# State-space stage: three sums per step made by DMAs that add to their destination

## The chip, the cores and the metric

The kernel runs on one core of a Trainium2 chip. It is one launch. The metric is the time of the launch in microseconds of the device, as the median of several runs. Five engines work side by side, each through its own queue of instructions in order: PE (TensorE, matrix products), DVE (VectorE), ACT (ScalarE), POOL (GpSimd) and SP (SyncE, which here only issues DMAs). 16 DMA engines move data between DRAM and the on-chip memory.

## The reference

Two layers over 1024 latent tokens and 256 context tokens of 1024 features, all float32. The first layer is a diagonal state-space mixer in both directions, the second an attention; each is followed by a SwiGLU block. The change lies in the mixer:

```python
def s5_direction(u, h0, ar, ai, bbr, bbi, C_re, C_im, reverse, want_y):
    ug = u.reshape(Bn, L, S5_G, S5_GC).swapaxes(0, 1)      # 64 groups of 16 features
    br = jnp.einsum('lbgc,gpc->lbgp', ug, bbr)             # 64 complex states a group
    bi = jnp.einsum('lbgc,gpc->lbgp', ug, bbi)
    ...                                                    # the state h0 of the context enters
    _, _, hr, hi = lax.associative_scan(s5_combine, (a_r, a_i, br, bi), reverse=reverse, axis=0)
    y = (jnp.einsum('lbgp,gcp->blgc', hr, C_re) - jnp.einsum('lbgp,gcp->blgc', hi, C_im))
```

## The kernel before

Features lie on the partitions, tokens along the free axis. Tokens are taken in blocks of eight: 160 blocks, J = 160, the first 32 of them context. Within a block the mixer is a matrix product; from block to block it is a scan of complex states. The complex scan is made a real one: the block inputs are turned back by the angle of their block (tables "tcs" and "tsn", cosine and sine), scanned with a real factor, and the states are turned forward again.

The loop of the stage has 32 steps (NS5) of two groups, both directions. A step n works at several depths at once:

- PE makes the block inputs of step n + 2 (`in_products`, tile psA, from the tokens "ug" and the input stack "bt").
- DVE runs the six scans of step n (`scans`: tile "zz" from "ww"), then turns the inputs of step n + 2 (`in_turn`: the products "pc" and "pq" of psA with the two tables), does one pass on the tables of step n + 3 (`ty`), turns the states of step n forward (`turn_back`: "qc", "qs") and makes the output stack "sc" of step n + AHEAD, AHEAD = 8 (`stack_out`: two products "sc", "su" and their difference).
- POOL adds pc and pq to "ww" (`in_sum`) and makes the input stack "sb" of step n + 4 (`stack_in`: two products "sb", "su" and their sum).
- ACT makes the tables (`tables_a`, `tables_c`: "ty", "tn", "tsn", "tcs"), and copies what PE wrote (`out_copy`: "gy"; `turned`: "bt").
- PE makes the outputs of step n - 1 (`out_products`, from qc, qs, sc, its swapped copy "cw", "ug" and "mt"), and transposes sb of step n + 3 (`turned`).
- SP loads and stores; every fourth step it loads the tokens ug of the next four steps (`load_u`), into one of two buffers.

The scan of the second direction needs the first column of ww behind the last one as well. Therefore ww has J + 1 columns, and ACT copies that pad column after POOL's sum:

```python
    def in_sum(pq):
        w = gt.tile([128, 4, J + 1], F32, name="ww", bufs=NW)
        add(w[:, :, :J], pq[0], pq[1], Q)
        copy(w[:, 1::2, J:J + 1], w[:, 1::2, 0:1])
```

From the first step on, the five queues keep the order in which the program is written (`pinned.update("VSQTD")`; V, S, Q, T, D are DVE, ACT, POOL, PE and SP). Before the loop a scheduler sets the order. All engine instructions are issued through one wrapper, so the profile shows the same line, L197, for all of them; they are told apart by the names of their tiles.

Of the kernel before, what the change touches and what calls it, by code (L numbers as in the profile page):

```python
"""Hybrid S5 / latent-attention trunk: two layers, one launch.

Everything is kept feature-major (features on partitions, tokens on the free
axis), so that no activation is ever transposed between products.  Tokens are
ordered (token-in-block t = 0..7, block j): 32 context blocks, then 128 latent
blocks, which gives the state-space mixer its blocks of eight tokens.

Float32 products with long moving operands are carried as three passes over
an exact two-part split of both operands (12 + 12 significant bits).
"""  # L10
# [46 lines left out]
# ---------------------------------------------------------------- host layout  # L57
def _units(w):
    """[K, N] -> [N/128][128 p][K/128 * 128]: one contiguous block per output tile."""
    k, n = w.shape  # L60
    return np.ascontiguousarray(
        w.reshape(k // 128, 128, n // 128, 128).transpose(2, 1, 0, 3)).reshape(n // 128, 128, k)
# [7 lines left out]
def _rope_rows():  # L70
    """cos and signed sin for the 32 rotary rows, for the latent tokens in kernel order."""
# [13 lines left out]
def _constants():  # L85
# [3 lines left out]
    steps = np.stack([j, np.where(j < JC, JC - 1 - j, J - 1 + JC - j)]).astype(np.float32)  # L89
    k["idx"] = np.broadcast_to(steps.reshape(1, 2 * J), (128, 2 * J))  # L90
# [91 lines left out]
# -------------------------------------------------------------------- device  # L182
def trunk(tc, I, out, dbg=None):
# [4 lines left out]
    class Engine:  # L188
        """an engine whose instructions keep the order of the program while pinned"""
# [31 lines left out]

    def split(h, l, x):
        """x -> (h, l): h = x rounded to 12 bits, l = the rest, both exact."""
        S.activation(h, x, AF.Copy)
        V.tensor_tensor(l, x, h.bitcast(F32), op=ALU.subtract)

    def split_in(h, l, e):
        """l holds the f32 values; split in place"""
        l32 = l.bitcast(F32)
        copy(h, l32)  # L230
        sub(l, l32, h.bitcast(F32), e)
# [43 lines left out]
    class Weights:  # L275
        """The weights of a sequence of products, loaded and split ahead of their use, in blocks
        of up to four tiles [128, 128].  A spec is ((one matrix [128, n * 128],), n), taken whole,
        or ((two of them), n), taken block by block in the order of `seven`."""
# [42 lines left out]
        def combined(self, s, j, w):  # L321
            """a11, a12, s2, a22, s3, s1, s4 with s1 = a21 + a22, s2 = s1 - a11, s3 = a11 - a21,
            s4 = a12 - s2"""
# [23 lines left out]
    def weights(specs):  # L347
        """a function that returns the weights in turn"""
        ws, ns = Weights([((ap,), n) for ap, n in specs]), iter(specs)
        return lambda: ws.whole(next(ns)[1])  # L350

    def mm3(outs, w, xs, nk, ks=None):
        """outs[n] += sum_k w[k]^T x[k][n], float32 in three passes; xs(k, n) -> (h, l)."""
# [7 lines left out]
    # ---------------------------------------------------------- constants  # L361
# [48 lines left out]
    def single(pst):  # L410
        """one bank after the other of the tiles of pst"""
        while True:
            t = pst()
            for n in range(t.shape[1]):
                yield t[:, n]

    # ------------------------------------------------------------- norms
# [3 lines left out]
    def rstd_of(acc, dim, ncol, nsub, pst, r=None):  # L421
        """1/sqrt(mean of squares + eps) per token on every partition; acc holds the squares,
        summed over feature tiles"""
# [15 lines left out]
    # a value that the next norm waits for  # L439
    behind_of = []  # L440

    def modnorm(p, xs, ncol, nsub, ranges, l, half, put, pst, nb=3, spare=None, order=range(8)):
        """in pieces: four for the squares, one for the mean, eight for the features;
        with eight spare tiles, in place and without memory of its own"""
# [30 lines left out]
    def put_seven(p, h, new, w):  # L475
        """of the tiles ft and ft + 4, halved along the tokens: b11, t1, b21, b22, t2, t3, -t4 with
        t1 = b12 - b11, t2 = b22 - t1, t3 = b22 - b12, t4 = t2 - b21"""
# [21 lines left out]
    # the products of `seven`: which of the combinations of put_seven takes part  # L499
# [27 lines left out]
    # ================================================ layer 0: S5 mixer  # L527
# [21 lines left out]
    def mod_first(st):  # L549
        """shift and scale of the first norm, on the tensor engine"""  # L550
# [26 lines left out]
    def discretise(st):  # L577
# [12 lines left out]
        def tanh_exp(o, x):  # L590
            """exp(x) = (1 + tanh(x/2)) / (1 - tanh(x/2))"""
# [62 lines left out]
        for o, x in zip(cpw, (pr, pi)):  # L654
            copy(by_d(o, 0), by_d(x, 0)[:, 1:9])
            V.tensor_copy(by_d(o, 1), by_d(x, 1)[:, 8:0:-1])
# [42 lines left out]
    def w_in_norm(p, xc):  # L699
        """normalised in place; in pieces"""  # L700
# [67 lines left out]
    idx = const("idx", 2 * J, sp)  # L768
# [16 lines left out]
    AHEAD = 8  # L785

    def stack(k, name, p_, x1, x2, op, e, p, nb):
        """for two groups, both directions: powers times coefficients"""
# [8 lines left out]
        u = ge.tile(sh, F32, name="su", tag="su" + name, bufs=1)  # L797
# [3 lines left out]
        e.tensor_tensor(a, a, u, op=op)  # L801
        return a.rearrange("p g t c -> p g (t c)")

    def stack_in(k):
        """with B-bar"""
        k0 = 4 * k
        sbs[k] = stack(k, "sb", bp, bb1[:, k0:k0 + 4], bb2[:, k0:k0 + 4], ALU.add, Q, ge, 2)

    def stack_out(k):
        """with C"""  # L810
        c = coef[k // 2][:, :, 4 * (k % 2):4 * (k % 2) + 4]
        scs[k] = stack(k, "sc", cpw, c[:, 0], c[:, 1], ALU.subtract, V, gp, 10), c[:, 0]

    def swap(k):
        """the latter with its halves swapped"""
# [6 lines left out]
    def turned(k):  # L822
        """the former, transposed; the lag kernels, by four groups"""
# [28 lines left out]
    def lag_out(q):  # L852
        """the products within a block"""
# [12 lines left out]
    def load_u(ft):  # L866
        ug = gp.tile([128, 8, J], F32, name="ug")
        dma(ug, ubd[ft].rearrange("t c g j -> (t c) g j"))
# [4 lines left out]
    NPC, NW, NGY = 2, 2, 2  # L873
    sh4 = [128, 4, J]

    def tables_a(n):
        """turns of two groups, both directions"""
        ty = wp.tile([128, 1024], F32, name="ty", tag="wr")[:, :4 * J].rearrange("p (a b) -> p a b", a=4)
        tn = wp.tile([128, 1024], F32, name="tn", tag="wb", bufs=6)[:, :4 * J].rearrange("p (a b) -> p a b", a=4)
        for i in range(4):  # L880
            S.activation(ty[:, i], idx[:, (i % 2) * J:(i % 2) * J + J], AF.Copy, scale=f8[:, 4 * n + i:4 * n + i + 1])
# [7 lines left out]
    def tables_c(n):  # L889
        """rotation tables"""  # L890
        ty, tn = tys.pop(n)
        tcs = gp.tile(sh4, F32, name="tcs", bufs=4)
        tsn = gp.tile(sh4, F32, name="tsn", bufs=4)
        trig(tcs, tsn, ty, tn, sg[:, 2:3])
        tab[n] = tcs, tsn

    def beside(m):
# [4 lines left out]
        if m == 4:  # L902
            for k in range(2):
                stack_in(k)
                stack_out(k)
                turned(k)
# [3 lines left out]
        if m == 6:  # L910
            for k in range(2, 4):
                stack_in(k)
                stack_out(k)
            turned(2)
# [8 lines left out]
        if m == 7:  # L923
            for k in range(4, AHEAD):
                stack_out(k)

# [4 lines left out]
    def in_products(n):  # L931
        """inputs of two groups (both directions) to the block states"""
        bt, ug = bts.pop(n), ugs[n // 4]
        va = []
        for sw in range(2):
            v = psA()
            for i in range(4):
                T.matmul(v[:, i // 2, (i % 2) * J:(i % 2) * J + J], bt[:, i, 64 * sw:64 * sw + 128],
                         ug[:, (2 * n + i // 2) % 8], start=True, stop=True)
# [3 lines left out]
    def in_turn(n, va):  # L943
        """rotated"""
        pq = []
        for v, t, nm in zip(va, tab[n], ("pc", "pq")):
            p_ = gt.tile(sh4, F32, name=nm, tag=nm, bufs=NPC)
            mul(p_.rearrange("p (g d) j -> p g (d j)", g=2), v[:, :, :2 * J],
                t.rearrange("p (g d) j -> p g (d j)", g=2))
            pq.append(p_)  # L950
        return pq

    def in_sum(pq):
        w = gt.tile([128, 4, J + 1], F32, name="ww", bufs=NW)
        add(w[:, :, :J], pq[0], pq[1], Q)
        copy(w[:, 1::2, J:J + 1], w[:, 1::2, 0:1])
# [5 lines left out]
    def scans(n, w, z):  # L962
        """over the blocks"""
# [5 lines left out]
        for i in (1, 3):  # L969
            scan(z[:, i, 0:JC - 1][:, ::-1], w[:, i, 1:JC][:, ::-1], i, 0.0)  # L970
        for i in (0, 2):
            scan(z[:, i, 1:J], w[:, i, 0:J - 1], i, 0.0)
        for i in (1, 3):
            scan(z[:, i, JC:J][:, ::-1], w[:, i, JC + 1:J + 1][:, ::-1], i, z[:, i, 0:1])

    def turn_back(n, z):
        qc = gt.tile(sh4, F32, name="qc", bufs=2)
        qs = gt.tile(sh4, F32, name="qs", bufs=2)
        mul(qc, z, tab[n][0])
        mul(qs, z, tab[n][1])  # L980
        return qc, qs

    def out_products(n, rot):
# [3 lines left out]
        for gi in range(2):  # L987
            o = py[:, gi * J:gi * J + J]
            T.matmul(o, mt[:, (2 * n + gi) % 4], ug[:, (2 * n + gi) % 8], start=True, stop=False)
# [18 lines left out]
    # steps of two groups; a step works on its scans, on the inputs two steps ahead, on the tables  # L1008
    # three steps ahead, on the stacks three and four steps ahead, and on the outputs one behind
    NS5 = 32  # L1010
    pend = {}
    for n in range(2):
        pend[n] = in_sum(in_turn(n, in_products(n)))
    rot = None
    pinned.update("VSQTD")
    for n in range(NS5 + 1):
# [16 lines left out]
        if n + 2 < NS5:  # L1033
            pq = in_turn(n + 2, va)
# [10 lines left out]
        if n + 4 < NS5:  # L1045
            stack_in(n + 4)
        if n + AHEAD < NS5:
# [3 lines left out]
        if n + 2 < NS5:  # L1051
            pend[n + 2] = in_sum(pq)
# [20 lines left out]
    def raw_y(ft):  # L1073
        """in the place of the residual stream"""
# [10 lines left out]
    # ==================================== layer 0: GLU, out projection  # L1085
# [7 lines left out]
    # the other modulation rows: on the vector engine, from rows of mod_w^T  # L1093
# [103 lines left out]
    # ============================================================== FFN  # L1197
# [681 lines left out]
```

## Time and profile before

| | before |
|---|---|
| runs | 3453.87, 3454.31, 3463.31 us |
| median | 3454.31 us |
| span of the profiled execution | 3461.5 us |
| PE busy | 3205.4 us (93%) |
| DVE busy | 2857.2 us (83%) |
| ACT busy | 1746.7 us (50%) |
| POOL busy | 1107.7 us (32%) |
| stage with the loop, 187 to 524 us | 337 us: DVE 331.1, PE 243.7, POOL 216.6, ACT 169.3 us busy |

The profile gives for the profiled execution its span, from the first to the last instruction, and no further time of its own. Shares over the whole span are shares over stages that differ: outside the loop PE is nearly always busy (2812.8 of the 2937 us behind it), inside it is not. So the stage is read by itself.

### The profile page before, as it was taken

The page shows a single profiled execution, that of the slowest core. Times are in us where ns is not written, and L with a number is a line of the kernel's source. Part 1 is how long each engine was busy: PE and PEld are TensorE (multiplying, and loading weights), DVE is VectorE, ACT ScalarE, POOL GpSimd, SP SyncE. Part 2 cuts the span into 40 slices and gives each one's busy share as a digit, 9 for nine tenths or more (in the row PEclk, how much of TensorE's full clock was granted, in tenths as well). Part 3 has the DMA queues.
Part 4 walks back from the last instruction along what each step waited for, and adds up shares of the span by engine and source line. Part 5 has one row for each costly group of instructions (what it writes and reads, how often), then busy time and mean ns, then how long its engine had stood idle before and what let it go on. Part 6 is the DMA issues. An engine that isn't in the chain of part 4 may idle for free. (4 is left out here: it accounts for less than half of the span.)

```text
span 3461.5 us, 55186 instructions
## 1 busy us (share of the span) xinstructions
PE 3205.4 (93%) x20468; PEld 2944.4 (85%) x20468; DVE 2857.2 (83%) x4672; ACT 1746.7 (50%) x3242; POOL 1107.7 (32%) x780
## 2 busy tenths in 40 slices
PE   6877679999999999999999989998999899999999
PEld 5876679999999999999987767777777699889998
DVE  6999996878788889888876668888886688898887
ACT  5455554324333444334465557777775444454443
POOL 2466650000111212113134345555554421221111
PEclk8988889999999999999999999999999999999999
DMA  7323236653333332322244752222225433333332
GB/s 257 108 74 79 69 81 217 226 176 116 104 110 100 105 113 92 127 83 75 87 156 135 201 151 69 78 79 74 75 72 136 138 104 104 98 104 110 104 106 78
DMA packets 175388, 395.78 MB, mean 114 GB/s; under 512 B 21200, under 2 KB 64144, under 8 KB 174096
## 3 DMA queue, kind: packets, MB, share of 16 engines
q1 hardware_dynamic: 175120, 392.26, 36.4%
q8 instruction: 161, 2.64, 0.3%
q14 instruction: 107, 0.88, 0.1%
HBM read 326.89 MB, written 53.49 MB: 110 GB/s over the span
## 5 line engine op out<-in xcount | busy, mean ns | idle before, releaser
L197 PE MATMUL psB<-hs,wb 128*128 128x320 f32 (+1 forms) x7392 | 1000.1, 297 | 24.0 <-DVE wb L197 16.4
L197 PEld LDWEIGHTS psB<-hs,wb 128*128 128x128 f32 x7392 | 989.8, 189 | 33.1 <-DVE wb L197 20.9
L197 ACT ACTIVATE wb<-wr 128x512 fp32r<-128x512 f32 (+3 forms) x704 | 405.5, 594 | 464.6 <-PE psB L197 220.3
L197 DVE TENSOR_TENSOR wb<-wr,wb 128x512 fp32r<-128x512 f32 (+3 forms) x704 | 494.7, 713 | 167.6 <-ACT wb L197 166.7
L197 PE MATMUL psB<-hb,wb 128*128 128x320 f32 (+1 forms) x3360 | 603.1, 340 | 15.5 <-ACT hb L197 8.4
L197 POOL TENSOR_TENSOR ws<-wr 128x512 f32<-128x512 f32 x176 | 245.5, 1400 | 1146.9 <-DMA wr<-in_fi 510.8
L197 PEld LDWEIGHTS psB<-hb,wb 128*128 128x128 f32 x3360 | 544.6, 188 | 69.6 <-ACT hb L197 10.5
L197 ACT ACTIVATE wb<-ws 128x512 fp32r<-128x512 f32 x352 | 218.9, 627 | 268.3 <-PE psB L197 193.2
L197 POOL TENSOR_TENSOR pl<-pf,ph 128x512 fp32r<-128x512 f32 x192 | 250.6, 1305 | 260.1 <-DVE ph L197 255.4
L197 DVE TENSOR_TENSOR wb<-ws,wb 128x512 fp32r<-128x512 f32 x352 | 273.7, 782 | 30.7 <-ACT wb L197 29.0
L197 PE MATMUL psA<-ha,wb 128*128 128x320 f32 x1680 | 249.1, 310 | 4.4 <-ACT ha L197 4.4
L197 PEld LDWEIGHTS psA<-ha,wb 128*128 128x128 f32 x1680 | 248.1, 189 | 5.0 <-ACT ha L197 4.6
L197 PE MATMUL psS<-kt,qt 128*128 128x512 f32 x768 | 213.4, 403 | 1.3 <-ACT p L197 1.3
L197 PEld LDWEIGHTS psT<-ident,p 128*128 128x128 f32 x1280 | 147.7, 140 | 72.6 <-issue 20.4
L197 PE MATMUL psT<-ident,p 128*128 128x128 f32 x1280 | 189.9, 275 | 20.5 <-DVE pl L197 17.5
L197 PE MATMUL psA<-ug,bt 128*128 128x160 f32 x512 | 111.0, 390 | 83.7 <-DVE pc L197 59.3
L197 PEld LDWEIGHTS psA<-ug,bt 128*128 128x128 f32 x512 | 102.7, 261 | 86.1 <-ACT kt L197 45.1
L197 DVE TENSOR_REDUCE mx<-psS 128x1 f32<-128x1024 f32 x128 | 155.6, 1215 | 19.7 <-PE psS L197 19.1
L197 PEld LDWEIGHTS psS<-kt,qt 128*128 128x128 f32 x768 | 140.1, 190 | 29.4 <-ACT p L197 2.3
L197 POOL TENSOR_TENSOR acc<-acc,sq 128x640 f32<-128x640 f32 (+1 forms) x51 | 83.0, 1627 | 243.5 <-ACT sq L197 204.6
L197 ACT ACTIVATE p<-psS,mx,scq 128x1024 f32<-128x1024 f32 x128 | 153.9, 1203 | 0.0
L197 PE MATMUL psO<-ph,vt 128*128 128x512 f32 x320 | 139.6, 436 | 2.5 <-DVE ph L197 0.4
(339 smaller groups left out, 5684.4 us busy)
## 6 DMA issues: line engine op xcount, KB each, us to landing
wr<-in_fi SPq DMA_DIRECT2D x176, 512.0 KB
wr<-in_mt SPq DMA_DIRECT2D x80, 512.0 KB
wr<-in_swg SPq DMA_DIRECT2D x32, 512.0 KB
wr<-in_fo SPq DMA_DIRECT2D x64, 256.0 KB
wr<-in_fo SPq DMA_DIRECT2D x32, 384.0 KB
kdr<-big SPq DMA_DIRECT2D x32, 320.0 KB
kt<-kdr SPq DMA_DIRECT2D x16, 640.0 KB
wr<-in_fo SPq DMA_DIRECT2D x32, 320.0 KB
```

What stands on the lines that cost most here:

```text
L197: r = f(*a, **k)
```

## The change

Three sums of a step are no longer instructions of DVE and POOL but DMAs that add the source to what the destination holds. They are issued by POOL. The sums are ww (pc + pq), sb and sc. The products go straight into the tile that receives the sum: pc becomes ww. A list `owed` collects the pairs, and `settle` issues them at one place in the step, behind POOL's two products. For sc the difference becomes a sum, since the sign goes into the table "cpi" ahead of the loop.

ww has no pad column any more. Instead the tokens ug get one (161 columns a group, `JX`), as do the tables; the products of the second direction read columns 1 to 160. ACT copies that column once per load of ug, that is every four steps, instead of once per step in ww. The two scratch tiles "su" get two buffers each, ww three; AHEAD falls from 8 to 6 and sc has 8 buffers instead of 10.

```diff
+    def gather(o, a):
+        Q.dma_start(o, a, accum_op=ALU.add)
...
-        for o, x in zip(cpw, (pr, pi)):
-            copy(by_d(o, 0), by_d(x, 0)[:, 1:9])
-            V.tensor_copy(by_d(o, 1), by_d(x, 1)[:, 8:0:-1])
+        for o, x, k in zip(cpw, (pr, pi), (1.0, -1.0)):
+            S.activation(by_d(o, 0), by_d(x, 0)[:, 1:9], AF.Copy, scale=k)
+            ts(by_d(o, 1), by_d(x, 1)[:, 8:0:-1], k, 0.0, ALU.mult, ALU.add)
...
-    AHEAD = 8
+    AHEAD = 6
+
+    owed = []
+
+    def settle():
+        for o, a in owed:
+            gather(o, a)
+        owed.clear()
...
-        u = ge.tile(sh, F32, name="su", tag="su" + name, bufs=1)
+        u = ge.tile(sh, F32, name="su", tag="su" + name, bufs=2)
         a = p.tile(sh, F32, name=name, tag=name, bufs=nb)
         mul(a, pw(p_[0]), cf(x1), e)
         mul(u, pw(p_[1]), cf(x2), e)
-        e.tensor_tensor(a, a, u, op=op)
+        owed.append((a.rearrange("p g t c -> p (g t c)"), u.rearrange("p g t c -> p (g t c)")))
...
     def load_u(ft):
-        ug = gp.tile([128, 8, J], F32, name="ug")
-        dma(ug, ubd[ft].rearrange("t c g j -> (t c) g j"))
+        ug = gp.tile([128, 8, JX], F32, name="ug")
+        dma(ug[:, :, :J], ubd[ft].rearrange("t c g j -> (t c) g j"))
+        copy(ug[:, :, J:JX], ug[:, :, 0:1])
         return ug
...
-                T.matmul(v[:, i // 2, (i % 2) * J:(i % 2) * J + J], bt[:, i, 64 * sw:64 * sw + 128],
-                         ug[:, (2 * n + i // 2) % 8], start=True, stop=True)
+                d = i % 2
+                T.matmul(v[:, i // 2, d * J:d * J + J], bt[:, i, 64 * sw:64 * sw + 128],
+                         ug[:, (2 * n + i // 2) % 8, d:d + J], start=True, stop=True)
...
-    def in_sum(pq):
-        w = gt.tile([128, 4, J + 1], F32, name="ww", bufs=NW)
-        add(w[:, :, :J], pq[0], pq[1], Q)
-        copy(w[:, 1::2, J:J + 1], w[:, 1::2, 0:1])
+        owed.append(tuple(p_.rearrange("p a j -> p (a j)") for p_ in pq))
+        return pq[0]
...
         if n + 2 < NS5:
-            pq = in_turn(n + 2, va)
+            pend[n + 2] = states(in_turn(n + 2, va))
...
         if n + 4 < NS5:
             stack_in(n + 4)
+        settle()
         if n + AHEAD < NS5:
             stack_out(n + AHEAD)
...
-        if n + 2 < NS5:
-            pend[n + 2] = in_sum(pq)
```

The order of POOL's queue in the loop, one step of before, from its products on sb to the two clears of zz (bpr, bpi, bb are constant tables):

```order
L197 TENSOR_TENSOR sb<-bpr,bb_132 128x512 [waits PE_49]
L197 TENSOR_TENSOR su<-bpi,bb_133 128x512 [waits Pool_49]
L197 TENSOR_TENSOR sb<-sb,su 128x512 [waits Pool_49]
L197 TENSOR_TENSOR ww<-pc,pq 128x4x160 [waits DVE_49,Activation_49]
L197 MEMSET zz 128x2 [waits Activation_49]
L197 MEMSET zz 128x2
```

The same queue and place in the changed kernel:

```order
L198 TENSOR_TENSOR sb<-bpr,bb_132 128x512 [waits DMASW1_49,PE_49]
L198 TENSOR_TENSOR su<-bpi,bb_133 128x512
L198 DMA sc<-su 128x512 [waits DMAHW5_49,DMAHW6_49,DMASW5_49,DVE_49]
L198 DMA ww<-pq 128x640 [waits DVE_49]
L198 DMA sb<-su 128x512 [waits DMASW7_49,Pool_49]
L198 MEMSET zz 128x2 [waits Activation_49]
L198 MEMSET zz 128x2
```

Two of the four passes are gone, and the three adding DMAs stand behind the two that are left; the one of ww still waits for DVE, and the one of sc is that of the step before.

The order of ACT's queue in a step of before, from the last table of one step to the first of the next (the queue has the pad copy of ww in each step):

```order
L197 ACTIVATE tcs<-tn,hpi 128x640 [waits Activation_49]
L197 ACTIVATE ty<-idx,f_127 128x160 x4
L197 ACTIVATE tn<-ty,magic 128x640 [waits Activation_49]
L197 ACTIVATE gy<-psB 128x320 [waits PE_49]
L197 ACTIVATE bt<-psB 128x4x128 [waits PE_49]
L197 ACTIVATE bt<-psB 128x4x64
L197 ACTIVATE cc<-cc,sg 128x128 [waits DMAHW7_49]
L197 ACTIVATE ww<-ww 128x2 [waits Pool_49]
L197 ACTIVATE tn<-ty 128x640 [waits DVE_49]
```

The same queue of the changed kernel in a step with a load of ug (every fourth; the other steps read the same without the row of ug):

```order
L198 ACTIVATE tcs<-tn,hpi 128x2x322 [waits Activation_49]
L198 ACTIVATE ug<-ug 128x8 [waits DMAHW2_49,PE_49]
L198 ACTIVATE ty<-idx,f_127 128x161 x4
L198 ACTIVATE tn<-ty,magic 128x2x322 [waits Activation_49,Pool_49]
L198 ACTIVATE gy<-psB 128x320 [waits PE_49]
L198 ACTIVATE bt<-psB 128x4x128 [waits PE_49]
L198 ACTIVATE bt<-psB 128x4x64
L198 ACTIVATE kt<-psB 128x240 [waits DMAHW7_49,PE_49]
L198 ACTIVATE tn<-ty 128x2x322 [waits DVE_49]
L198 ACTIVATE tsn<-ty,sg 128x2x322
```

The pad copy of ww is gone from every step, and in every fourth step the copy of ug's pad column, which waits for a DMA and for PE, stands ahead of the four ty.

## Rows read from the trace of the kernel before

**Rows 1.** Busy time by stretch: start:end, length, engines (instructions), PEclk, DMA share, GB/s

```profile
300.00:400.00 100.00, 71.06 (x470) 68.02 (x468) 99.72 (x125) 51.26 (x116) 67.44 (x53) 0.83 0.28 69
```

**Rows 2.** Timeline of DVE, two steps: start us, us, engine, line, op, out<-in, count

```profile
302.33 0.79 DVE L197 TENSOR_TENSOR pc<-psA,tcs 128x640 f32<-128x640 f32 x1
...
304.51 2.15 DVE L197 TENSOR_TENSOR qc<-zz,tcs 128x640 f32<-128x640 f32 x1
...
311.63 0.69 DVE L197 TENSOR_TENSOR sc<-sc,su 128x512 f32<-128x512 f32 x1
312.24 1.09 DVE L197 TENSOR_TENSOR_SCAN zz<-r,ww 128x31 f32<-128x31 f32 x4
...
314.00 0.80 DVE L197 TENSOR_TENSOR pc<-psA,tcs 128x640 f32<-128x640 f32 x1
...
315.44 0.82 DVE L197 SCALAR_TENSOR_TENSOR ty<-tn,ty 128x640 f32<-128x640 f32 x1
316.17 0.82 DVE L197 TENSOR_TENSOR qc<-zz,tcs 128x640 f32<-128x640 f32 x1
...
318.97 1.92 DVE L197 TENSOR_TENSOR sc<-sc,su 128x512 f32<-128x512 f32 x1
320.81 3.96 DVE L197 TENSOR_TENSOR_SCAN zz<-r,ww 128x31 f32<-128x31 f32 x4
...
325.45 0.79 DVE L197 TENSOR_TENSOR pc<-psA,tcs 128x640 f32<-128x640 f32 x1
```

**Rows 3.** Timeline of POOL, the same two steps; in brackets the idle before and its releaser

```profile
304.00 1.99 POOL L197 TENSOR_TENSOR ww<-pc,pq 128x640 f32<-128x640 f32 x1 [2.69 <-DVE pq L197]
...
315.67 4.66 POOL L197 TENSOR_TENSOR ww<-pc,pq 128x640 f32<-128x640 f32 x1 [4.62 <-DVE pq L197]
...
321.81 1.10 POOL L197 TENSOR_TENSOR su<-bpi,bb 128x512 f32<-128x512 f32 x1
322.99 1.44 POOL L197 TENSOR_TENSOR sb<-sb,su 128x512 f32<-128x512 f32 x1
```

**Rows 4.** Timeline of DVE, a later step without work on sc: its two ends

```profile
473.89 0.79 DVE L197 TENSOR_TENSOR pc<-psA,tcs 128x640 f32<-128x640 f32 x1
...
483.43 0.79 DVE L197 TENSOR_TENSOR pc<-psA,tcs 128x640 f32<-128x640 f32 x1
```

**Rows 5.** Timeline of PE: first and last products of a step, first of the next

```profile
314.94 2.41 PE L197 MATMUL psA<-ug,bt 128*128 128x160 f32 x16 [2.67 <-DVE pc L197]
...
321.41 0.27 PE L197 MATMUL psB<-cc,bb 128*32 128x16 f32 x4
326.39 4.44 PE L197 MATMUL psA<-ug,bt 128*128 128x160 f32 x16 [4.70 <-DVE pc L197]
```

**Rows 6.** Timeline of ACT in the second of the two steps

```profile
320.37 0.21 ACT L197 ACTIVATE ww<-ww 128x2 f32<-128x2 f32 x1 [7.92 <-POOL ww L197]
...
322.54 1.37 ACT L197 ACTIVATE ty<-idx,f 128x160 f32<-128x160 f32 x4
...
324.68 0.42 ACT L197 ACTIVATE gy<-psB 128x320 f32<-128x320 f32 x1
```

**Rows 7.** Timeline of SP's queue: the load of ug

```profile
319.17 0.34 SPq L197 DMA_DIRECT2D ug<-ub  x1
```

**Rows 8.** DMA, 318 to 328 us: rate in 40 slices of 0.25 us; packets; busy share

```profile
GB/s 0 0 0 0 0 0 0 0 184 164 225 307 328 266 348 287 336 377 373 389 320 107 61 49 33 8 25 8 0 0 0 0 0 0 0 0 0 0 0 0
DMA packets 448, 1.05 MB, mean 105 GB/s; under 512 B 64, under 2 KB 192, under 8 KB 448
...
q1 hardware_dynamic: 448, 1.05, 31.7%
```

**Rows 9.** DMA, 246 to 254 us, with a store of gy in pieces of 640 B

```profile
DMA packets 1637, 1.12 MB, mean 140 GB/s; under 512 B 215, under 2 KB 1509, under 8 KB 1637
...
q1 hardware_dynamic: 1637, 1.12, 64.3%
```

**Rows 10.** Timeline of PE ahead of the loop: the first use of sc

```profile
149.31 0.69 PE L197 MATMUL psB<-sc,bb 128*32 128x112 f32 x4 [4.17 <-DVE sc L197]
```

More of the change, by code (lines that the diff above doesn't have):

```diff
@@ L88, in _constants @@
     j = np.arange(J)
-    steps = np.stack([j, np.where(j < JC, JC - 1 - j, J - 1 + JC - j)]).astype(np.float32)
-    k["idx"] = np.broadcast_to(steps.reshape(1, 2 * J), (128, 2 * J))
+    steps = np.stack([j, np.where(j < JC, JC - 1 - j, J - 1 + JC - j)])
+    steps = np.concatenate([steps, steps[:, :1]], axis=1).astype(np.float32)
+    k["idx"] = np.broadcast_to(steps.reshape(1, 2 * (J + 1)), (128, 2 * (J + 1)))
     dm = np.zeros((128, C16), np.float32)
@@ L766, in trunk @@
     close(st)
-    idx = const("idx", 2 * J, sp)
+    JX = J + 1
+    idx = const("idx", 2 * JX, sp)
     dmask = const("dmask", C16, sp)
@@ L784, in trunk, with stack @@
     sh = [128, 4, TB, C16]
-    AHEAD = 8
-    def stack(k, name, p_, x1, x2, op, e, p, nb):
+    AHEAD = 6
[4 more added lines that the diff above has]
+        owed.clear()
+    def stack(k, name, p_, x1, x2, e, p, nb):
         k0 = 4 * k
@@ L806, in stack_in @@
         k0 = 4 * k
-        sbs[k] = stack(k, "sb", bp, bb1[:, k0:k0 + 4], bb2[:, k0:k0 + 4], ALU.add, Q, ge, 2)
+        sbs[k] = stack(k, "sb", bp, bb1[:, k0:k0 + 4], bb2[:, k0:k0 + 4], Q, ge, 2)
     def stack_out(k):
         c = coef[k // 2][:, :, 4 * (k % 2):4 * (k % 2) + 4]
-        scs[k] = stack(k, "sc", cpw, c[:, 0], c[:, 1], ALU.subtract, V, gp, 10), c[:, 0]
+        scs[k] = stack(k, "sc", cpw, c[:, 0], c[:, 1], V, gp, 8), c[:, 0]
     def swap(k):
@@ L866, in load_u, with pairs, turns_in, turns_out @@
     def load_u(ft):
-        ug = gp.tile([128, 8, J], F32, name="ug")
-        dma(ug, ubd[ft].rearrange("t c g j -> (t c) g j"))
+        ug = gp.tile([128, 8, JX], F32, name="ug")
+        dma(ug[:, :, :J], ubd[ft].rearrange("t c g j -> (t c) g j"))
+        copy(ug[:, :, J:JX], ug[:, :, 0:1])
         return ug
     ugs, gys, tab, tys = {}, {}, {}, {}
-    NPC, NW, NGY = 2, 2, 2
+    NPC, NW, NGY = 2, 3, 2
     sh4 = [128, 4, J]
+    sht = [128, 2, 2 * JX + 2]
+    def pairs(t):
+        return t.rearrange("p g (d j) -> p g d j", d=2)[:, :, :, :J]
+    def turns_in(t):
+        return pairs(t)
+    def turns_out(t):
+        return pairs(t[:, :, :2 * JX])
     def tables_a(n):
-        ty = wp.tile([128, 1024], F32, name="ty", tag="wr")[:, :4 * J].rearrange("p (a b) -> p a b", a=4)
-        tn = wp.tile([128, 1024], F32, name="tn", tag="wb", bufs=6)[:, :4 * J].rearrange("p (a b) -> p a b", a=4)
+        def flat(t):
+            return t[:, :2 * sht[2]].rearrange("p (a b) -> p a b", a=2)[:, :, :2 * JX]
+        ty = flat(wp.tile([128, 1024], F32, name="ty", tag="wr"))
+        tn = flat(wp.tile([128, 1024], F32, name="tn", tag="wb", bufs=6))
         for i in range(4):
-            S.activation(ty[:, i], idx[:, (i % 2) * J:(i % 2) * J + J], AF.Copy, scale=f8[:, 4 * n + i:4 * n + i + 1])
+            l = slice((i % 2) * JX, (i % 2) * JX + JX)
+            S.activation(ty[:, i // 2, l], idx[:, l], AF.Copy, scale=f8[:, 4 * n + i:4 * n + i + 1])
         S.activation(tn, ty, AF.Identity, bias=magic)
@@ L891, in tables_c @@
         ty, tn = tys.pop(n)
-        tcs = gp.tile(sh4, F32, name="tcs", bufs=4)
-        tsn = gp.tile(sh4, F32, name="tsn", bufs=4)
-        trig(tcs, tsn, ty, tn, sg[:, 2:3])
+        tcs = gp.tile(sht, F32, name="tcs", bufs=4)
+        tsn = gp.tile(sht, F32, name="tsn", bufs=4)
+        trig(tcs[:, :, :2 * JX], tsn[:, :, :2 * JX], ty, tn, sg[:, 2:3])
         tab[n] = tcs, tsn
@@ L913, in beside @@
                 stack_out(k)
+                settle()
             turned(2)
@@ L925, in beside @@
                 stack_out(k)
+                settle()
     w_in_mm(1, h, beside)
@@ L945, in in_turn, with states @@
         pq = []
[L946 to L949, printed above, removed]
+        for v, t, nm in zip(va, tab[n], ("ww", "pq")):
+            p_ = gt.tile(sh4, F32, name=nm, tag=nm, bufs=NW if nm == "ww" else NPC)
+            mul(p_.rearrange("p (g d) j -> p g d j", g=2),
+                v[:, :, :2 * J].rearrange("p g (d j) -> p g d j", d=2), turns_in(t))
             pq.append(p_)
-        return pq
-    def in_sum(pq):
-        w = gt.tile([128, 4, J + 1], F32, name="ww", bufs=NW)
-        add(w[:, :, :J], pq[0], pq[1], Q)
-        copy(w[:, 1::2, J:J + 1], w[:, 1::2, 0:1])
+        owed.append(tuple(p_.rearrange("p a j -> p (a j)") for p_ in pq))
+        return pq[0]
+    def states(w):
         z = wp.tile([128, 1024], F32, name="zz", tag="wb", bufs=6)[:, :4 * J].rearrange("p (a b) -> p a b", a=4)
@@ L969, in scans @@
         for i in (1, 3):
-            scan(z[:, i, 0:JC - 1][:, ::-1], w[:, i, 1:JC][:, ::-1], i, 0.0)
+            scan(z[:, i, 0:JC - 1][:, ::-1], w[:, i, 0:JC - 1][:, ::-1], i, 0.0)
         for i in (0, 2):
@@ L973, in scans @@
         for i in (1, 3):
-            scan(z[:, i, JC:J][:, ::-1], w[:, i, JC + 1:J + 1][:, ::-1], i, z[:, i, 0:1])
+            scan(z[:, i, JC:J][:, ::-1], w[:, i, JC:J][:, ::-1], i, z[:, i, 0:1])
     def turn_back(n, z):
@@ L978, in turn_back @@
         qs = gt.tile(sh4, F32, name="qs", bufs=2)
-        mul(qc, z, tab[n][0])
-        mul(qs, z, tab[n][1])
+        for q, t in ((qc, tab[n][0]), (qs, tab[n][1])):
+            mul(q.rearrange("p (g d) j -> p g d j", g=2), z.rearrange("p (g d) j -> p g d j", g=2), turns_out(t))
         return qc, qs
@@ L988, in out_products @@
             o = py[:, gi * J:gi * J + J]
-            T.matmul(o, mt[:, (2 * n + gi) % 4], ug[:, (2 * n + gi) % 8], start=True, stop=False)
+            T.matmul(o, mt[:, (2 * n + gi) % 4], ug[:, (2 * n + gi) % 8, :J], start=True, stop=False)
             for d in range(2):
@@ L1012, in trunk @@
     for n in range(2):
-        pend[n] = in_sum(in_turn(n, in_products(n)))
+        pend[n] = states(in_turn(n, in_products(n)))
+        settle()
     rot = None
@@ L1046, in trunk @@
             stack_in(n + 4)
+        settle()
         if n + AHEAD < NS5:
```

## Prediction

> **What bounds the kernel now.** I first read the busy time of the engines by stretches to find the stage that the change touches, the state-space loop of 32 steps from 187 to 524 us. VectorE is busy 99.7 of 100 us there, PE 71, ScalarE 51, GpSimd 67, the DMA engines 28% [rows 1]. So VectorE's own queue sets the pace, and I read it instruction by instruction. From one product "pc" of a step to the one two steps on it takes 23.12 us, 11.56 us a step [rows 2]. It never idles, but not all of its busy time is work: the reader should compare rows of one shape. "qc" takes 0.82 us in one step and 2.15 in the other; the sum "sc" 0.69 and 1.92; the four scans 1.09 and 3.96 [rows 2]. The timeline of GpSimd for the same stretch shows what stands beside each long one: the sum "ww" beside qc in the one step and beside sc in the other, the three passes on "sb" and "su" beside the scans [rows 3]. GpSimd is held in the same way: its "ww" takes 1.99 us once and 4.66 once [rows 3]. Two-input passes of the two engines take turns. In the second step VectorE loses 1.23 us at ww and 2.87 at the three sb passes, 0.96 each; in the first it loses 1.33 at ww. I take 1.28 for ww and 0.96 for each sb pass.
>
> PE works 6.74 us of a step (314.94 to 321.68) and then waits for pc to free its PSUM tile [rows 5]. Behind an idle of 2.67 us its next 16 products take 2.41 us, behind one of 4.70 us 4.44 [rows 5]; the mean granted clock of the stage is 0.83 [rows 1]. ScalarE waits 7.92 us in the second step for GpSimd's ww, to copy the pad column [rows 6].
>
> **What goes.** Each step loses (1) the sum of sc on VectorE, 0.61 us from its start to the next start [rows 2], (2) GpSimd's sum ww, worth 1.28 us on VectorE, (3) GpSimd's sum on sb, worth 0.96. That is 2.85 us, and a step becomes 8.71 us. The look-ahead of the output stack falls from 8 to 6, so steps 24 and 25, which had no sc work (a step of 9.54 us against 11.45 [rows 4]), now have its two products. Sum: steps 0 to 23, 24 x 2.85 = 68.4; steps 24 and 25, 2 x (2.24 - 1.22) = 2.0; steps 26 and 27, 2 x 2.24 = 4.5; steps 28 and 29, which have no sb, 2 x 1.28 = 2.6. Together 77.5 us. Nothing else catches the time at 8.71: PE needs 6.74 at the higher of its two clock levels, and its idle of 2.0 us would be shorter than the 2.67 us after which it still ran at that level; ScalarE needs 0.51 x 11.56 = 5.9 us and no longer waits for ww. The tables grow by one column, 161 for 160; that is below what I can count.
>
> **What comes.** GpSimd issues three adding DMAs a step, in the order sc, ww, sb, behind its two products. The trace has no such DMA. The issue is bounded below by SP's 0.34 us for a DMA [rows 7] and above by a GpSimd pass of the same tile that was held, 4.66 us [rows 3]; I take 1.0, near the undisturbed pass of 1.10 [rows 3]. GpSimd then needs 3 x 1.0 for issues and about 2.7 for its two products, under 8.71. Landing: a batch of 1.05 MB is through 4.1 us after its issue [rows 7, 8]; for 0.26 to 0.33 MB I take 3 us. Whom does that delay? ww is issued behind pq and read by scans some 14 us later. sb is read by PE's transposes of the next step, on which PE has 2.0 us of slack and which feed products used only a step later. sc is read two steps later. So the landing is hidden, unless GpSimd's queue runs late (third rival).
>
> DMA load of a step: now 0.28 x 11.56 = 3.2 us of all 16 engines [rows 1]. The load of the inputs "ug" goes into rows of 161, so its pieces are 640 B: 1024 where there were 256. A piece of about 2.3 KB costs 113 ns (0.317 x 10 us x 16 / 448 [rows 8]), one of about 0.68 KB 50 ns (0.643 x 8 us x 16 / 1637 [rows 9]); that adds 0.35 us a step. The three sums move 384 pieces: 2.7 us as copies. Sum 6.3 of 8.71 us. If a piece that adds costs twice a copy, 9.0; three times, 11.7. I take a value between one and two, which does not decide. The Trainium skill (Collectives: The Full Stack, section "The bandwidth ceiling: the fold count and why AG ≠ RS ≠ AR") says that an adding transfer needs two source reads and so runs at half the rate of a copy; no run here shows it yet. By that rule the load is the 9.0 of the second rival.
>
> **The new wait.** Every fourth step ScalarE copies the pad column of the newly loaded ug, at the head of its work for the step, before the four "ty". This copy waits for the load, and the load waits until PE has read the old tile: it is issued 5.17 us after pc (319.17 against 314.00 [rows 2, 7]). Its batch starts to move 0.83 us after the issue and is through after 4.1 [rows 8]; ug alone in the new pieces takes 1024 x 50 ns / 16 = 3.2 us, so it lands 4.0 us after the issue if it runs alone, and 4.1 + 1.4 = 5.5 with what is issued behind it: 9.2 to 10.7 us after pc. From ty to the end of tn ScalarE needs 2.14 us [rows 6], the copy 0.2. VectorE wants the result 1.44 us behind the next pc [rows 2], at 8.71 + 1.44 = 10.15 us; it gets it at 11.5 to 13.0. That is 1.4 to 2.9 us, and up to 4.5 if the adding DMAs take half of the engines meanwhile; nothing, if PE and the load come earlier than I think. Behind the waiting copy stand ty, tn, gy and the two copies of bt, for which PE waits too; PE has time for it, since its products are one step ahead. I take 2.9 us x 6 loads (steps 4 to 24) = 17 us.
>
> Start: PE waited 4.17 us for the first sc [rows 10]. That sum is now a DMA behind GpSimd's queue, about 4 us (issue 1, landing 3) where VectorE took 0.6 to 1.5; the first scan likewise waits for ww by DMA. I take 5 us for both, between 0 and 8.
>
> **Sum.** 77.5 - 17 - 5 = 55 us less. The profiled execution has a span of 3461.5 us, 1.8 below the slowest of the three runs and 7.2 above their median; the difference carries over, so 3454.3 - 55 = 3399 us. The likeliest case by itself: 3380 to 3420.
>
> **Rivals.**
> 1. *The pad wait is hidden, and the two products left on GpSimd fall less on VectorE* (beside pc and pq, which read PSUM and stay at 0.80 us throughout [rows 2]). For it: GpSimd is released by pq, its products come at a new place. Against it: VectorE's other passes stand back to back. If one of the two products costs nothing, 26 x 0.96 = 25 us more, and 17 for the wait: 3357 us; a half of that, 3378.
> 2. *The DMA engines become the bound.* At twice the price of a copy a step is 9.0: 26 x 0.3 = 8 us, and the pad wait grows by some 2 us six times: 3419 us. At three times, 11.7 a step, the gain is gone and the pad wait stays: about 3480. For it: ug and the stores in pieces of 640 B already fill the engines in stretches (64% over 8 us [rows 9]). Against it: the present mean of 28%.
> 3. *Slower: GpSimd's queue becomes the bound.* The DMAs stand in order behind waits: from pq (1.45 us behind pc) the issues of ww and sb, two products (2.7), the issue of sc, its landing, and only then may VectorE write that su buffer again, two steps on, at 4.25 us behind pc. With an issue of D and a landing of L a step is at least 3D + L - 0.1. This decides from 3D + L = 8.8 and makes the kernel slower from 11.7. If the issue is held by VectorE as ww is (on the mean of 1.99 and 4.66 about 1.9 us over an undisturbed 1.4 [rows 3]), D is 2.9, and with L = 3.5 a step is 12.1: 26 x 0.54 = 14 us, the 22 us of waits beside it, 3490 us. For it: the held passes of rows 3. Against it: an issue reads no tile. The Trainium skill (SBUF — State Buffer, sections "SBUF: two separate sides" and "Who interferes with whom") says that GpSimd cannot write descriptors while VectorE is in a two-port mode, and infers that tensor_tensor does not do this. By that, D stays small here.
>
> **Chances.** Forecast 0.50; first rival 0.10; second 0.20, about half of it still clearly faster; third 0.20. Faster by over 0.3% (10 us, about what a measurement of this kernel tells from no change) 0.70, within 0.3% 0.09, slower 0.21. The range leaves out most of the third rival and the far end of the first: 3366 to 3465 us.
>
> **What would show it.** In the new timeline of VectorE: a step of 8.5 to 9 us in three of four, sc and su without a third pass, at most two lengthened instructions a step, and every fourth step an idle of 1 to 4 us before ty, released by ScalarE. On GpSimd two passes and three issues a step, the issues near 1 us. Wrong would be a VectorE that waits for a DMA before su or a scan in every step, issues of 2 us and more, or DMA engines near full in the stage; and a granted clock of PE that falls, with PE as the bound.

## The result and the profile after

| | before | changed |
|---|---|---|
| median of four runs each | 3454.2 us | 3407.0 us (3403.2 to 3410.1) |
| ratio to before, 95% interval | | 0.9855 (0.984 to 0.9871) |
| span of the profiled execution | 3461.5 us | 3403.6 us |
| last "pc" (now "ww") of the loop starts at | 507.88 us | 450.00 us |

The change is 1.4% faster. Between the profiled executions 57.9 us are gone, and all of them lie ahead of the last product from psA: behind its start both spans have 2953.6 us. That the two agree so well is partly chance, since this part takes 2945.6 to 2965.3 us in the ten profiled executions of this document.

The busy time of the stretch that [rows 1] shows of before, in the changed kernel:

```profile
300.00:400.00 100.00, 80.59 (x596) 77.35 (x596) 89.26 (x146) 66.31 (x141) 58.08 (x77) 0.85 0.89 182
```

VectorE is no longer always busy, and the DMA engines went from 0.28 to 0.89. VectorE's timeline has a step of each kind; the rows answer to [rows 2]:

```profile
293.76 2.98 DVE L198 TENSOR_TENSOR_SCAN zz<-r,ww 128x31 f32<-128x31 f32 x4
...
297.42 0.79 DVE L198 TENSOR_TENSOR ww<-psA,tcs 128x640 f32<-128x640 f32 x1
...
303.24 0.83 DVE L198 SCALAR_TENSOR_TENSOR ty<-tn,ty 128x644 f32<-128x644 f32 x1 [4.29 <-ACT tn L198]
...
306.80 1.09 DVE L198 TENSOR_TENSOR_SCAN zz<-r,ww 128x31 f32<-128x31 f32 x4
...
308.56 0.80 DVE L198 TENSOR_TENSOR ww<-psA,tcs 128x640 f32<-128x640 f32 x1
...
317.09 0.79 DVE L198 TENSOR_TENSOR ww<-psA,tcs 128x640 f32<-128x640 f32 x1
```

From 308.56 to 317.09 is a normal step, 8.53 us. From 297.42 to 308.56 is one with a load of ug, 11.14 us: VectorE stands 4.29 us ahead of ty. The scans take 2.98 us in one step and 1.09 in the other. GpSimd's timeline, which answers to [rows 3], shows why:

```profile
290.73 0.86 POOL L198 DMA_DIRECT2D ww<-pq  x1 [2.33 <-DVE pq L198]
291.27 1.21 POOL L198 DMA_DIRECT2D sb<-su  x1
...
291.90 2.94 POOL L198 TENSOR_TENSOR sb<-bpr,bb 128x512 f32<-128x512 f32 x1
294.81 1.09 POOL L198 TENSOR_TENSOR su<-bpi,bb 128x512 f32<-128x512 f32 x1
295.85 0.85 POOL L198 DMA_DIRECT2D sc<-su  x1
...
300.42 1.78 POOL L198 TENSOR_TENSOR sb<-bpr,bb 128x512 f32<-128x512 f32 x1
301.48 1.77 POOL L198 TENSOR_TENSOR su<-bpi,bb 128x512 f32<-128x512 f32 x1
...
307.18 0.88 POOL L198 DMA_DIRECT2D sc<-su  x1 [3.93 <-DVE zz L198]
```

In the normal step GpSimd's two products end beside the scans; in the long one they run at 300.42 to 303.25, while VectorE waits, and cost it nothing. What VectorE waits for is at the head of ScalarE's queue, as [rows 6] shows it for before; this is ScalarE's timeline:

```profile
300.78 0.22 ACT L198 ACTIVATE ug<-ug 128x8 f32<-128x8 f32 x1 [7.39 <-DMA ug<-ub]
```

and this the issue of the load in the timeline of SP's queue ([rows 7] for before):

```profile
295.01 0.57 SPq L198 DMA_DIRECT2D ug<-ub  x1
```

The load is issued at 295.01 and lets the copy go 5.8 us later. PE falls back with it ([rows 5] for before):

```profile
304.06 4.63 PE L198 MATMUL psA<-ug,bt 128*128 128x160 f32 x16 [5.93 <-DVE ty L198]
...
313.24 2.44 PE L198 MATMUL psA<-ug,bt 128*128 128x160 f32 x16
```

Behind an idle of 5.93 us its 16 products take 4.63 us, a step later 2.44. The DMA view of 300 to 400 us, with its issues (KB each, median us from issue to landing), in place of [rows 8, 9]:

```profile
q0 software_dynamic: 4694, 9.26, 51.9%
q1 hardware_dynamic: 12099, 8.88, 36.7%
...
ww<-pq POOLq DMA_DIRECT2D x11, 320.0 KB, 4.1
sb<-su POOLq DMA_DIRECT2D x11, 256.0 KB, 6.3
...
sc<-su POOLq DMA_DIRECT2D x11, 256.0 KB, 4.5
```

q0 holds the adding DMAs: 0.519 x 100 us x 16 / 4694 = 177 ns a piece.

### The profile page after: what moved, and what is told of

Same layout as the page of the kernel before. It is cut to its first block, busy times and chain, and to the rows that moved or that the text cites. A ratio compares the mean times of both kernels' runs of the same rounds, so it can differ in the third digit from the quotient of the medians.

```text
span 3403.6 us, 55331 instructions
## 1 busy us (share of the span) xinstructions
PE 3181.9 (93%) x20468; PEld 2922.9 (86%) x20468; DVE 2760.2 (81%) x4640; ACT 1745.4 (51%) x3218; POOL 1032.8 (30%) x812
## 5 line engine op out<-in xcount | busy, mean ns | idle before, releaser
L198 ACT ACTIVATE hb<-sg 128x640 fp32r<-128x640 f32 (+1 forms) x104 | 72.0, 693 | 147.8 <-DVE sg L198 147.4
L198 DVE TENSOR_TENSOR ws<-ws,wr 128x512 f32<-128x512 f32 x88 | 89.2, 1014 | 60.3 <-POOL ws L198 56.6
```

The costliest lines, as they stand in the source:

```text
L198: r = f(*a, **k)
```

## The experiments

Because the part behind the loop varies that much, the table gives beside the ratio the mean step of the loop: from the third to the 29th product from psA with tcs ("pc" of before, "ww" of the others), 26 steps.

| kernel | median us | ratio to before (95%) | third, 29th start | mean step |
|---|---|---|---|---|
| before | 3454 to 3459 | | 186.87, 483.43 | 11.41 |
| changed | 3407.0 | 0.9855 (0.9840 to 0.9871) | 187.60, 428.48 | 9.27 |
| pad_late | 3385.7 | 0.9789 (0.9776 to 0.9802) | 188.83, 413.53 | 8.64 |
| undo_ww | 3434.6 | 0.9930 (0.9918 to 0.9943) | 185.45, 458.70 | 10.51 |
| undo_sb | 3424.1 | 0.9909 (0.9895 to 0.9924) | 188.93, 455.78 | 10.26 |
| undo_sc | 3413.4 | 0.9869 (0.9855 to 0.9884) | 185.86, 440.55 | 9.80 |
| pad_dram | 3390.4 | 0.9804 (0.9790 to 0.9817) | 189.26, 413.72 | 8.63 |
| copy_not_add | 3379.7 | 0.9776 (0.9763 to 0.9790) | 185.50, 407.02 | 8.52 |
| extra_gather | 3412.1 | 0.9871 (0.9853 to 0.9889) | 188.84, 431.60 | 9.34 |
| one_product | 3382.0 | 0.9783 (0.9770 to 0.9796) | 186.81, 398.96 | 8.16 |

**pad_late: the pad copy one step later.**

```diff
-        copy(ug[:, :, J:JX], ug[:, :, 0:1])
         return ug
...
             tables_a(n + 3)
+        if n % 4 == 1 and n + 3 < NS5:
+            pad_u(ugs[n // 4 + 1])
```

(`pad_u` is the same copy; for the first ug it is made ahead of the loop.)

> The changed kernel with the copy of ug's pad column one step later, behind the four ty and the tn of that step. Theory (the wait for the load at the head of ScalarE's work is what each fourth step loses): the six long steps of 11.5 us fall to 8.6, 6 x 2.84 = 17 us less than the changed kernel, about 3390 us, and VectorE no longer idles before ty. Rival (the DMA engines, 87 to 89% busy in the stage, are the bound behind it: without the pauses they would be asked for more than they have): at most 5 us less, about 3402, with waits for adding DMAs in place of the idle before ty.

The six long steps are gone, and one step of 9.47 us is left, in which VectorE does not wait; the mean step falls by 0.62 us, 16.2 us over the 26, and the two intervals do not touch. ScalarE waits for the load nowhere, and VectorE and the DMA engines are both full:

```profile
300.00:400.00 100.00, 83.01 (x657) 78.32 (x656) 100.00 (x157) 67.48 (x140) 62.61 (x83) 0.95 0.96 198
```

The wait, and not the burst of transfers, made the long steps. PE's granted clock rises from 0.85 to 0.95 with it.

**undo_ww: the sum ww again a pass of GpSimd.**

```diff
         for o, a in owed:
-            gather(o, a)
+            if o.shape[-1] == 4 * J:
+                add(o, o, a, Q)
+            else:
+                gather(o, a)
```

> The changed kernel with the sum ww back as a pass of GpSimd, at the place of its DMA; sb and sc stay DMAs. Theory (VectorE loses 1.28 us a step to that pass): 24 free steps x 1.28 = 31 us more than the changed kernel, up to 38 if the long steps lose it too: 3438 to 3445 us. Rival (the load of the adding DMAs is what holds the step): a third less of that load gives back part of it and shortens the pad wait, 3420 to 3428.

The time is 3 us under the range that the theory gave, the mean step is 1.25 us longer than that of the changed kernel, and both hide what happened. VectorE's timeline of two steps:

```profile
305.38 4.94 DVE L198 TENSOR_TENSOR_SCAN zz<-r,ww 128x31 f32<-128x31 f32 x4
...
311.00 0.79 DVE L198 TENSOR_TENSOR ww<-psA,tcs 128x640 f32<-128x640 f32 x1
...
313.28 1.55 DVE L198 SCALAR_TENSOR_TENSOR ty<-tn,ty 128x644 f32<-128x644 f32 x1 [0.76 <-ACT tn L198]
314.75 3.16 DVE L198 TENSOR_TENSOR qc<-zz,tcs 128x640 f32<-128x640 f32 x1
```

The wait for the load in the second of them, in ScalarE's timeline:

```profile
310.82 0.22 ACT L198 ACTIVATE ug<-ug 128x8 f32<-128x8 f32 x1 [5.81 <-DMA ug<-ub]
```

The scans take 4.94 us instead of 2.98, and every step takes 10.1 to 10.9 us. The load still keeps ScalarE waiting, but in a longer step that costs VectorE 0.76 us here and 6.5 in all six loads of the 26 steps, against 25.8 in the changed kernel. Against pad_late, where VectorE does not wait for a load, a step costs 10.51 - 8.64 = 1.87 us more; 6.5 / 26 = 0.25 of it is that wait. The scans show the price of the pass by itself: 4.94 - 2.98 = 1.96.

**undo_sb: the sum sb again a pass of GpSimd.**

```diff
-        owed.append((a.rearrange(...), u.rearrange(...)))
+        if e is Q:
+            add(a, a, u, Q)
+        else:
+            owed.append((a.rearrange(...), u.rearrange(...)))
```

> The changed kernel with the sum on sb back as a pass of GpSimd right behind its two products. Theory: 0.96 us a step on VectorE in 22 to 28 steps, 21 to 27 us more than the changed kernel, 3428 to 3434 us. Rival (DMA load): PE no longer waits for the landing of sb, and the pad wait shrinks; under 12 us more, below 3420.

The time lies between the two ranges, 4 us below that of the theory; the mean step is 1.00 us longer, near the 0.96 of the prediction. The scans of a step show the third held pass, 4.01 us for the 2.98 above:

```profile
305.87 4.01 DVE L198 TENSOR_TENSOR_SCAN zz<-r,ww 128x31 f32<-128x31 f32 x4
```

Here the wait for the load stays: VectorE stands 27.5 us for the six loads, against 25.8 in the changed kernel.

**undo_sc: the sum sc again a pass of VectorE** (as above, with `e is V` and `V`).

> The changed kernel with the sum sc back as a pass of VectorE. Theory: 0.61 us in each of 26 steps, 16 us more, 3423 us; in the long steps too, since VectorE does it itself. Rival (the pass is worth more, because GpSimd's products then fall at another place, or less, because a third of the adding load is gone): 3410 or 3435.

In time between the two theories, and the interval overlaps that of the changed kernel. In the loop it is clear: 9.80 for 9.27, 0.53 us a step, where a pass of 0.61 was put back. The missing 0.08, 2.1 us over the 26 steps, is near what the pad wait gives: the six waits take 20 us for 25.8, while the six ty behind them are lengthened by 5.3 us in all for 2.0. The loop ends 10.6 us later than in the changed kernel (460.57 for 450.00), the span only 2.6 us: 8 us came back behind the last product. What makes that part vary stays open.

**pad_dram: the pad column written with the stores.**

```diff
-ubd = [dp.tile([TB, C16, 8, J], ...
+ubd = [dp.tile([TB, C16, 8, J + 1], ...
...
+            copy(ut[:, :, J:J + 1], ut[:, :, 0:1])
...
-        dma(ug[:, :, :J], ubd[ft].rearrange("t c g j -> (t c) g j"))
-        copy(ug[:, :, J:JX], ug[:, :, 0:1])
+        dma(ug, ubd[ft].rearrange("t c g j -> (t c) g j"))
```

> The pad column is written once, when the inputs are stored to DRAM (rows of 161), and comes back with the load as one piece of 5152 bytes a partition; ScalarE makes no pad copy in the loop. If the wait of that copy for the load of ug is all that made every fourth step long, the long steps go as they do with the copy moved one step later, and the time is the same as there within 5 us: 3380 to 3391. If the copy that was moved later still costs something (its 0.3 us on ScalarE, or the 1024 pieces of 640 bytes of a load), it comes out lower, 3370 to 3379. If the long steps have another cause (the burst of transfers in them), they stay, and the time is 3400 to 3410.

The first answer: a mean step of 8.63 as in pad_late, by another way. That the load has fewer pieces is worth nothing that shows.

**copy_not_add: the three DMAs copy** (pad_late with `Q.dma_start(o, a)`; the three sums are left out).

> As the version with the pad copy one step later, but the three DMAs of a step copy instead of adding (the three additions are left out). The price of adding is read from the time a piece takes: 177 ns in the changed kernel against 113 ns in the copies of the kernel before, another shape. If the adding itself costs, a piece falls to 90 to 125 ns here and the share of the DMA engines from 0.94 to 0.70 to 0.80; if the price comes from the shape (partition to partition, 2 to 2.5 KB), it stays at 160 to 180 ns. If VectorE alone bounds the loop (100% busy in 300 to 400 us), the time stays at 3380 to 3390 either way; if the engines at 0.94 hold it too, it falls to 3360 to 3375.

The stretch of 300 to 400 us by engines:

```profile
300.00:400.00 100.00, 80.03 (x657) 74.33 (x657) 100.00 (x160) 67.70 (x145) 62.57 (x80) 1.00 0.68 202
```

and the queue of the three DMAs in the same stretch (packets, MB, share of 16 engines):

```profile
q0 software_dynamic: 2868, 10.16, 27.1%
```

I had asked for the time of a piece. It is 151 ns, in neither of my ranges, and that was the wrong unit: the copies go in fewer, larger pieces (3.5 KB for 2.0). By bytes it is plain. A copy holds the engines 0.271 x 1600 / 10.16 = 43 us per MB; adding does so in pad_late for 0.549 x 1600 / 9.72 = 90 us per MB:

```profile
q0 software_dynamic: 4945, 9.72, 54.9%
```

That is 2.1 times as long. Fuller engines are not the reason: in undo_ww, at a DMA share of 0.63, adding takes 0.286 x 1600 / 5.04 = 91 us per MB as well. Of the adding step of a collective the Trainium skill (Collectives: The Full Stack, section "The bandwidth ceiling: the fold count and why AG ≠ RS ≠ AR") says that it needs two source reads and runs at half the rate of the copying one; the ratio measured here agrees with the two. That the second read is the reason is not shown: the adding DMAs also go in smaller pieces, and no run separates the two. Pieces of 2.3 KB alone did not cost it in the load of [rows 8], 0.317 x 160 / 1.05 = 48 us per MB, but that load comes from DRAM.

The time falls by 6 us against pad_late, where I gave 0 or 10 and more; the intervals overlap. The mean step falls by 0.12 us: the adding costs little, and VectorE is always busy in both runs.

**extra_gather: a fourth adding DMA in each step** (pad_late with the output stack of one step added to the next, which changes the sums).

```diff
             stack_in(n + 4)
+            if n + AHEAD - 2 < NS5:
+                o, a = (scs[n + AHEAD - k][0].rearrange("p a b -> p (a b)") for k in (2, 3))
+                owed.append((o, a))
         settle()
```

> As the version with the pad copy one step later, with a fourth adding DMA of 256 KB in each step (the output stack of one step ago is added to the next one, which changes the sums). By 142 pieces of 177 ns on 16 engines it adds 1.6 us of load to a step that has 8.1 of 8.6 us already. If the DMA engines are the next bound, a step becomes 9.5 to 9.9 us and the time 3408 to 3425. If there is more room than the busy share shows, only the issue on GpSimd (0.5 to 1.2 us, which VectorE does not wait for) is added: 3380 to 3392.

The same two views of this run:

```profile
300.00:400.00 100.00, 78.18 (x592) 73.94 (x590) 92.67 (x140) 61.49 (x129) 64.66 (x87) 0.91 1.02 206
```

```profile
q0 software_dynamic: 6009, 11.66, 66.7%
```

The share of 1.02 reads as full engines, and the time is 26 us above that of pad_late, 18 of it in the 26 steps. The mean step, 9.34, misses the 9.5 that was the least for a bound by DMA alone. From 200 to 300 us VectorE is still 98.6% busy with steps of 9.5 and 8.5 us in turn: GpSimd's two products lengthen kt, sc and su by 2.7 us together in the long ones (264.56 to 268.72) and the scans by 1.9 in the short ones. Only the later part, with VectorE at 92.7%, waits. The run shows that there is no room for a fourth, and not which of the two takes more of it.

**one_product: GpSimd makes one product less** (pad_late with a constant tile in place of the second product of sb, which is left out).

> As the version with the pad copy one step later, without the second of GpSimd's two products of a step (the sum takes a constant tile in its place). By the lock of 0.96 us that each pass of GpSimd costs VectorE, a step goes from 8.6 to 7.6 us and the time to 3355 to 3362. If the DMA engines (8.1 us of load a step) bound there, a step stops at 8.1 to 8.3 and the time at 3370 to 3380. If the lock costs nothing by pass but only by the work that VectorE has beside it, nothing moves: 3383 to 3389.

VectorE's timeline in a step:

```profile
310.49 2.02 DVE L198 TENSOR_TENSOR_SCAN zz<-r,ww 128x31 f32<-128x31 f32 x4
...
315.03 0.82 DVE L198 TENSOR_TENSOR ww<-psA,tcs 128x640 f32<-128x640 f32 x1 [1.77 <-ACT tcs L198]
```

and the stretch of 300 to 400 us:

```profile
300.00:400.00 100.00, 80.70 (x657) 76.66 (x656) 92.46 (x161) 68.40 (x145) 50.52 (x71) 0.97 0.98 201
```

Both answers are in it. With one pass the scans take 2.02 us for 2.98, so one held pass is 0.96, and a step without a long wait is 7.56 to 7.72. But the DMA engines are at 0.98, and in the same stretch ScalarE waits for loads (view of the waits: us in total, times, longest us):

```profile
ACT ug L198 <- DMA ug<-ub: 9.8, 3, 4.0
...
ACT cc L198 <- DMA cc<-in_c: 8.4, 2, 6.1
```

and so does PE:

```profile
PE psB L198 <- DMA mt<-kd: 8.6, 3, 3.8
```

The mean step is 8.16, what the second theory gave, and the time 3382, 2 us above its range and not told apart from pad_late by the intervals. The loop ends 15.5 us earlier than in pad_late (419.25 for 434.78), the time is only 3.7 us less, so most of the gain does not reach it. The waits point to the DMA engines as the next bound, close behind VectorE; a run with one product and copies in place of the adds would tell, and was not made.

pad_late beats both kernels and computes all of the reference: 2.1% under before, 0.7% under the changed kernel.

## Why the prediction was right

The direction, the mechanism and the place were right; 3407 lies 8 us above the 3399 forecast, inside its range.

- **What goes.** Forecast: 8.71 us a normal step, 77.5 us in all. The normal steps are 8.51 to 8.79. Without the new wait (pad_late) the 26 steps of the table lose 296.56 - 224.70 = 71.9 us, where the working gave 24 x 2.85 + 2.0 = 70.4 for them. No run took back by itself what else the change has (the look-ahead of 6, the third buffer of ww, the pad copy that is gone from every step), so their part in it is not shown. The split was less good than the sum: sc 0.53 for 0.61, sb 1.00 for 0.96, ww 1.25 beside the pad wait for 1.28, but 1.87 without it. So ww, put back, costs nearly two held passes of 0.96, not one and a third. The three do not simply add up, since each was undone with the other two in place and with another pad wait (6.5 us in undo_ww, 20 in undo_sc, 27.5 in undo_sb, 25.8 with none undone); how they divide when all are taken out together stays open.
- **Held passes.** The two products left cost 1.9 us in a step (2.98 against 1.09 for the scans), 0.96 a pass by one_product. The Trainium skill (SBUF — State Buffer, section "Who interferes with whom") says that a pass of VectorE with two inputs in SBUF contends with one of GpSimd that reads there. The rows agree: the passes that were lengthened are scans, qc, qs, kt, sc, su and ty, none of which reads psA, and those on psA stay at 0.79 to 0.83. The first rival had the two products fall beside those; it did not happen.
- **The new wait.** Forecast 2.9 us six times, 17 in all. pad_late puts it at 16.2 us over the 26 steps. The size came out right by two errors that cancel: VectorE stands 25.8 us in six (3.0 to 5.8 each, 4.3 on the mean, at the far end of the 1.4 to 4.5), since the load shown is issued 6.1 us after the product (295.01 against 288.90, for 5.2) and is through after 5.8; but in five of the six GpSimd's two products fall into that idle and give 1.9 back: 25.8 - 9.5 = 16.3.
- **DMA.** The load of the engines is 0.89 of a stretch of long and short steps, and 0.96 x 8.64 = 8.3 us a step in pad_late, between the 6.3 of the copy price and the 9.0 of the double. The price by bytes did double; the start of the sum was too high: 2.7 us for the three as copies, where copy_not_add shows 0.271 x 8.52 = 2.3. Adding they take 0.549 x 8.64 = 4.7. So the second rival was some 4% away, and extra_gather reaches it. The 0.35 us a step for ug in pieces of 640 B was too much as well: with ug in whole rows (pad_dram) the share of the engines stays at 0.95 for 0.96.
- **Issues.** Taken as 1.0 us; they take 0.85 to 1.21, and those of ww and sb start 0.54 us apart. The third rival, held issues of 2.9 us, did not occur: no issue was lengthened in these rows. Landings are 4.1 to 6.3 us instead of 3. VectorE waits for them only at the start and in its last scans; PE waits 4.7 us in all for sb from 300 to 400 us, where it is not the bound.
- **Start.** 5 us forecast. The first scan, in VectorE's timeline, waits 5.28 us for its sum:

```profile
185.84 1.09 DVE L198 TENSOR_TENSOR_SCAN zz<-r,ww 128x31 f32<-128x31 f32 x4 [5.28 <-DMA ww<-pq]
```

  PE waits 3.28 us for the first sc, less than the 4.17 of [rows 10]:

```profile
148.13 0.54 PE L198 MATMUL psB<-sc,bb 128*32 128x112 f32 x4 [3.28 <-DMA sc<-su]
```

  The first product from psA comes 2.9 us earlier (176.38 for 179.29), and the third is 0.7 us late (187.60 for 186.87), so 0.7 in place of 5. The wait of the first scan alone is as long as the forecast for both; that it cost so little is luck, since PE made its first products earlier.
- **End.** Forecast 4.5 + 2.6 us for steps 26 to 29. From the 29th product to the last, 24.45 us became 21.52, so 2.9: near the end VectorE waits 0.32 and 0.66 us for PE and 1.55 for kt. Behind the last product the last scans wait for their sum, so there the landing is not hidden:

```profile
458.80 1.09 DVE L198 TENSOR_TENSOR_SCAN zz<-r,ww 128x31 f32<-128x31 f32 x4 [2.33 <-DMA ww<-pq]
```

  What the start had too much and the end too little is about the same, so the sum of the spans came out by luck here.
- **Where the 8 us are.** In the spans the forecast was 55 us and 57.9 came: 55.7 in the 26 steps (forecast 70.4 - 17 = 53.4) and 2.9 at the end, less 0.7 at the start. The step that failed is "the difference carries over": the profiled execution of before, 3463.3 us, lies 9.1 us above the median of its runs, that of after, 3405.4 us, 1.6 below. That is 10.7 us of spread that I had carried as if it were a constant. It is of the size by which the part behind the loop varies; where the time goes in runs without a profile no run shows.

## What to carry to other kernels

A sum taken off two engines that hold each other is worth the held passes as well as its own; count them by comparing rows of one shape. Put an instruction that waits for a load behind the work of its step that others need, not at the head of the queue: here the same small copy one step later was worth 16 us in the loop and 21 in the medians. When DMAs take over work, add up the engines' busy time at the double price for the ones that add: the next thing saved on the compute engines may be paid back there.

## What the hardware showed beyond that

- An adding DMA of 128 rows of 2 to 2.5 KB from tile to tile held the DMA engines for 90 us per MB (pad_late), a plain copy of the same tiles for 43 (copy_not_add).
- GpSimd issued three such DMAs a step in 0.85 to 1.21 us each, two of them 0.54 us apart; in pad_late VectorE ran without a break from 300 to 400 us beside them.
- Taking 0.96 us of held pass from each step (one_product) shortened the step of the loop to 7.56 us at its best and 8.16 on the mean; beside the longer steps stand waits of ScalarE and PE for loads.
